# The first products, the step sizes, the memory tokens and the attention pieces of a hybrid decoder step, put in another order

## The chip, the cores and the metric

The kernel runs on one core of one Trainium2 chip. The metric is the device time of one execution in microseconds (us). The core has TensorE (PE, the matrix engine, with its weight loads PEld), VectorE (DVE), ScalarE (ACT), GpSimd (POOL) and SyncE (SP), which here only issues DMA transfers. ACT issues some transfers too. Each engine works through its own instructions in order, and waits at an instruction until what it reads or overwrites is free.

## The reference

One layer of a decoder is computed for 1024 prompt tokens and 8 sample tokens, all in fp32. One normalised input goes through one wide projection; its columns feed three mixers whose results are gated and summed.

```python
def mixer_block(xn, mem_k, mem_v, ...):
    sc_b, sc_c, sc_x, z, xbc, dt_raw, q, gates = jnp.split(xn @ w_in, splits, axis=-1)
    conv_u, sc_new = causal_depthwise_conv(sc_c * sc_x, sc_hist, sc_conv_w)
    y_a = (sc_b * conv_u) @ w_sc_out
    xbc_c, ssm_conv_new = causal_depthwise_conv(xbc, ssm_hist, ssm_conv_w)
    xbc_c = jax.nn.silu(xbc_c + ssm_conv_b)
    xs, bm, cm = jnp.split(xbc_c, ...)
    dt = jax.nn.softplus(dt_raw + ssm_dt_bias)
    a = -jnp.exp(ssm_a_log)
    y_ssd, ssm_new = ssd_fn(xs, dt, a, bm, cm, ssm_s0)
    y_ssd = (y_ssd + ssm_d[:, None] * xs) * jax.nn.silu(z)
    y_b = group_rmsnorm(y_ssd, ssm_norm_w, SSM_GROUPS) @ w_ssm_out
...
```

The third mixer is cross-attention of 4 heads of 256 into 256 memory tokens; for the prompt, keys and values are projected from the normalised `mem_prompt`, for the samples they come from a cache. `xbc` has 24 blocks of 128 columns: 16 of x, four B (block 16 is "B0") and four C (block 20 is "C0"). `dt_raw` has 32 columns, one step size for each head.

## The kernel before

Tokens lie along the free dimension, TT = 1032 = 1024 + 8, features along the 128 partitions. A factor is kept as a high part in the matmul's format and a low part (`weights`, `split_act`), and a product is the sum hi·hi, hi·lo, lo·hi. `gemm` makes one block of 128 output columns from 8 blocks of input as 72 matmuls of 344 columns (rows with L203 in the profile). A pair of blocks can instead be made by Strassen's scheme (`strassen`, matmuls of 258 columns at L248, results named Z2m, X17m, G16m and so on); it needs sums of blocks of the activations (`make_forms`) and of the weights, and splits each into high and low parts: a weight sum such as X17sa is made on DVE in two steps (L315, L316) and cast on ACT (X17Sh, L235).

The instructions are written by functions in program order and then ordered by a scheduler with its own estimates of their durations. Within a `gemm` or a Strassen pair small pieces of other work are issued: the queue `pend` holds them, and `tick` takes one out; `pace` says how many are taken in one gemm. `flush` issues what is left. Tiles come from pools with a fixed number of buffers: three raw weights, five wide tiles in the pool "ev" (`ev_tile`), two PSUM banks for small results (`sm_ps`). A load into a buffer waits until the last reader of the old contents is done, and on SP's queue everything behind it waits too.

The stages that the change touches, in order of time:

- **First phase** (loop at L507). Blocks of x are squared, transposed (ps_xt), scaled into `xw` and split into `xn`. `first_products(g3, k)` (L489) adds block k of the column group g3 to two results at once: ps_dt, the step sizes before the bias (128 weight columns, of which 32 are wanted), and ps_B0. Three products each make 24 matmuls per block row and 72 for each result. Weight blocks are loaded ahead of x3 to x7.
- **Histories** (L522 to L533). The convolution states are loaded and turned by 32 small transposes (ps_h) into `h_xc` and `h_sc`.
- **C0, B0, z0.** dtr takes ps_dt plus the bias on DVE (L553). `xbc_tile(16, "B0")` evicts ps_B0 and starts its convolution; C0 is a gemm of its own inside `xbc_tile(20)`; then `z_step(0)`. Into these gemms five pieces of `pend` are put: a gap, `dt_softplus` (nine transposes ps_dtT, then some twenty DVE steps of 288 columns), `dt_sums` (ps_ac), `dt_rows` (ps_acT, stores to DRAM) and `dt_sample` (ps_ex).
- **Memory tokens.** They are loaded into "ev" tiles, squared on ACT, scaled on DVE (L1172), transposed (ps_mt, L1179) and split in `mem_t`. `kv_block` makes keys and values in 16 pieces inside z1 and the pairs Z2 to Z12; they are stored to k_d and v_d in DRAM.
- **Later pairs**: X17, X18, X19 with B and C blocks, then X and gate pairs, into which `with_steps` puts slots of the sample's recurrence; at the end z_pair(14) and gate_pair(16) with slots, then gate_pair(18), (20), (22).
- **The SSD stage** (groups 0 to 3), with the query products and the first output products as `fillers` and `outs`. `group_norm` ends each group (psny at L1049, psnr, yb_d stores at L1076).
- **Attention**, as pieces within the output products po13 to po27 (`out_part`, one gemm each). `kv_in(m)` loads vv and kk from v_d and k_d and turns kk (pskT). `a_load`, `a_scores` (psa), `a_probs` (psp), `a_out` (psv) work on the prompt's heads. For the samples `s_query`, `s_keys`, `s_scores` take eight samples through DVE, five slots of pieces for each; after the last head come `s_softmax` (pss_sc), `s_probs` (pss_pT), for each sample `s_values` (two loads vc of 512 KB) and `s_out` (pso, 32-column stationary tiles on four column groups, L1484; then a copy so and four stores to os_d), four `conv_state` pieces, and `s_back` (osr, psob, a store into at_d). Then po30 starts, which reads all of at_d back (`in`, cast to b00h at L162).

## Time and profile before

| what | us |
|---|---|
| times of three runs | 2502.51, 2506.6, 2508.41 (median 2506.6) |
| profiled execution, its own time | 2510.98 |
| its span | 2509.3 |
| TensorE busy | 2463.0 |
| VectorE busy | 1518.3 |
| ScalarE busy | 1047.5 |
| mean granted TensorE clock, first phase (0 to 62.44) | 0.99 of full |
| the same, 62.44 to 77.18 | 0.83 of full |

In rows of the timeline the columns are start, duration, engine, line, operation, output <- inputs, shapes and how many were put together (x8); in square brackets stands how long the engine sat idle before it and what ended that. fp32 matmuls other than the split products leave two records each. Matmuls overlap, so the pitch from one start to the next tells more than the duration of one.

### The profile page before, as it was taken

Reading aid. Unit: us, or ns where it says so; the run is one execution under the profiler, and the core shown is the slowest. Engines: PE = TensorE matmul, PEld = TensorE weight load, DVE = VectorE, ACT = ScalarE, POOL = GpSimd, SP = SyncE. Lnnn points to the kernel's source line nnn. Section 1 sums busy time; section 2 is a strip of 40 time slices with the busy share of each in tenths; the row PEclk is TensorE's granted clock in tenths of the full one; section 3 lists DMA queues with packets and bytes.
Section 4 is the critical chain, followed back from the end, with each engine's and each line's share of the span. In section 5 each row is a group of like instructions: output and inputs, shape, how many; then the busy total and the mean of one; then the engine's idle time right before and its main releaser. Section 6 shows DMA issues by size and latency. Waiting matters only on the chain.

```text
span 2509.3 us, 44975 instructions
## 1 busy us (share of the span) xinstructions
PE 2463.0 (98%) x18762; PEld 2398.2 (96%) x18762; DVE 1518.3 (61%) x2484; ACT 1047.5 (42%) x1694; POOL 128.2 (5%) x163
## 2 busy tenths in 40 slices
PE   7999999999999999999999999999999999999998
PEld 5999999999999999999898998899999999999998
DVE  6754586777677764567786672555775445453325
ACT  6554455454545534655554541223443333341212
POOL 0300000000000000211211000000000000000000
PEclk9999999999999999999999999999999999999999
DMA  6344434344344445677886787945443222282211
GB/s 199 112 144 156 131 102 145 110 141 125 98 135 135 130 132 165 194 231 264 264 282 208 242 291 239 305 151 173 136 152 98 89 68 85 81 278 88 68 34 68
DMA packets 348331, 392.08 MB, mean 156 GB/s; under 512 B 15335, under 2 KB 285783, under 8 KB 348120
## 3 DMA queue, kind: packets, MB, share of 16 engines
q1 hardware_dynamic: 327678, 331.50, 42.3%
q10 hardware_dynamic: 20449, 57.71, 6.0%
q8 instruction: 147, 2.41, 0.4%
q14 instruction: 57, 0.46, 0.1%
HBM read 280.40 MB, written 108.98 MB: 155 GB/s over the span
## 4 chain that ended last, share of the span: by engine, by line
PE 89%; DMA 4%; DVE 2%; ACT 2%; issue 1%; SPq 0%; ACTq 0%; POOL 0%; DVEq 0%
PE po L203 13%; PE pd L203 9%; PE pm L1693 4%; PE ps_q L203 2%; PE pss L949 1%; PE py L936 1%; PE po L928 1%; PE ps_z L203 1%; PE u20m L248 1%; PE C3m L248 1%; PE Z6m L248 1%; PE g20m L248 1%; PE u18m L248 1%; PE g18m L248 1%; PE u16m L248 1%
## 5 line engine op out<-in xcount | busy, mean ns | idle before, releaser
L1835 DVE TENSOR_TENSOR x<-pd,x 128x1032 f32<-128x1032 f32 x24 | 29.6, 1232 | 134.4 <-PE pd L203 134.3
L881 ACT ACTIVATE r<-r,acum 128x128 f32<-128x128 f32 x256 | 78.9, 392 | 5.7 <-DMA r<-ac_d 5.2
L661 DVE SCALAR_TENSOR_TENSOR ax<-u,prm,ax 128x1024 f32<-128x1024 f32 x44 | 56.3, 1280 | 0.1
L913 POOL TENSOR_TENSOR xdd<-xdt,decst 128x512 f32<-128x512 f32 x32 | 36.2, 1130 | 320.7 <-DVE xdt L909 320.7
L822 ACT ACTIVATE st<-st,es 128x128 f32<-128x128 f32 x128 | 42.0, 394 | 23.5 <-DMA st<-in_state_ssm_dram 21.7
L1340 DVE TENSOR_TENSOR yr<-po,yr 128x1032 f32<-128x1032 f32 x8 | 9.8, 1230 | 58.7 <-PE po L203 54.6
L907 DVE TENSOR_TENSOR r<-r,cbm 128x1024 f32<-128x1024 f32 x32 | 39.1, 1223 | 2.3 <-ACT r L882 0.2
L824 DVE SCALAR_TENSOR_TENSOR st<-sr,dts,st 128x128 f32<-128x128 f32 x128 | 40.1, 345 | 0.4
L932 DVE TENSOR_TENSOR y<-po,ea 128x512 f32<-128x512 f32 x28 | 19.3, 688 | 28.0 <-PE po L928 25.1
L828 DVE SCALAR_TENSOR_TENSOR sr<-st,sr 128x128 f32<-128x128 f32 x128 | 35.4, 286 | 1.1
L949 PE MATMUL pss<-xdd,bT 128*128 128x512 f32 x64 | 34.2, 616 | 1.0 <-ACT bT L906 0.8
L936 PE MATMUL py<-r,xdt 128*64 128x128 f32 x512 | 35.0, 279 | 0.0
L882 ACT ACTIVATE r<-r 128x1024 f32<-128x1024 f32 x32 | 33.9, 1059 | 0.6
L962 POOL TENSOR_TENSOR s<-s,cdec 128x512 f32<-128x512 f32 x28 | 33.1, 1181 | 2.5 <-DVE s L955 2.2
L1700 DVE TENSOR_TENSOR x<-pm,xT 128x516 f32<-128x516 f32 x16 | 11.1, 695 | 36.3 <-PE pm L1693 36.3
L906 ACT COPY bT<-bp 128x128 f32<-128x128 f32 x32 | 8.5, 265 | 54.8 <-DVE cbm L904 54.7
L936 PEld LDWEIGHTS py<-r,xdt 128*64 128x64 f32 x512 | 27.3, 136 | 4.2 <-issue 0.9
L928 PE MATMUL po<-bc,s 128*128 128x128 f32 x224 | 29.9, 276 | 0.0
L1622 DVE TENSOR_TENSOR gt<-po,gt 128x1032 f32<-128x1032 f32 x8 | 9.9, 1233 | 32.8 <-PE po L203 31.8
L928 PEld LDWEIGHTS po<-bc,s 128*128 128x128 f32 x224 | 28.2, 191 | 0.7 <-DVE s L955 0.5
L1073 DVE SCALAR_TENSOR_TENSOR x<-x,prm,sqa 128x1032 f32<-128x1032 f32 x16 | 19.6, 1290 | 15.0 <-ACT sqa L1069 15.0
L664 DVE SCALAR_TENSOR_TENSOR ax<-u,prm,ax 128x1032 f32<-128x1032 f32 x22 | 28.3, 1287 | 0.0
(9205 smaller groups left out, 8974.3 us busy)
## 6 DMA issues: line engine op xcount, KB each, us to landing
r<-ac_d SPq DMA_DIRECT2D x32, 512.0 KB
gt_d<-G ACTq DMA_DIRECT2D x24, 516.0 KB
gt<-gt_d SPq DMA_DIRECT2D x24, 516.0 KB
xs_d<-ax ACTq DMA_DIRECT2D x22, 516.0 KB
hr<-h_d SPq DMA_DIRECT2D x22, 516.0 KB
x<-xs_d SPq DMA_DIRECT2D x16, 516.0 KB
zs<-zs_d SPq DMA_DIRECT2D x16, 516.0 KB
yb_d<-x SPq DMA_DIRECT2D x16, 516.0 KB
```

The costliest lines, as they stand in the source:

```text
L203: PE.matmul(ps[:, n, :CW], wt[:, ks], x[:, n * CW : (n + 1) * CW], start=(k == 0 and i == 0), stop=(k == nk - 1 and i == 2),)
L248: PE.matmul(ps[:, n, :HC], wt[:, ks], x[:, n * HC : (n + 1) * HC], start=(start and kt == 0 and i == 0), stop=(kt == 3 and i == 2), skip_g ...
L661: V.scalar_tensor_tensor(acc[:, :T], u[:, j : j + T], w[j], acc[:, :T], op0=ALU.mult, op1=ALU.add)
L822: S.activation(st[:, i], st[:, i], AF.Copy, scale=es[:, g * 4 + i, b : b + 1])
L824: V.scalar_tensor_tensor(st[:, i], rb, dts[:, g * 4 + i, b : b + 1], st[:, i], op0=ALU.mult, op1=ALU.add)
L881: S.activation(r[:, j, :], r[:, j, :], AF.Relu, scale=-1.0, bias=acum[:, c, h : h + 1])
L907: V.tensor_tensor(r, r, bc(cbm.unsqueeze(1), [P, HPG, P]), op=ALU.mult)
L913: G.tensor_tensor(b3(xdd, HPG), b3(xdt, HPG), bc(decst[:, c, hs].unsqueeze(2), [P, HPG, 64]), op=ALU.mult)
L928: PE.matmul(po[:, t * P : (t + 1) * P], state["s"][:, t * P : (t + 1) * P], bcg[1][:, cs], start=True, stop=True,)
L936: PE.matmul(py[hp : hp + 64, (h // 2) * P : (h // 2 + 1) * P], xdt[:, h * 64 : (h + 1) * 64], r[:, (h % 2) * 4 + h // 2, :], start=True, s ...
L949: PE.matmul(pss, bT, xdd, start=True, stop=True)
L1693: PE.matmul(ps[:, n, :HC], wt[:, ks], x[:, half * HT + n * HC : half * HT + (n + 1) * HC], start=(k == 0 and i == 0), stop=(k == KD - 1 an ...
```

## The change

Eight edits, in the order of the kernel:

1. The first phase makes B0 and C0; the step sizes are made apart by `step_sizes`, from the raw fp32 weight and the unsplit `xw`: for each column group eight matmuls with 32 stationary columns, block k on the column group k mod 4 of the array, so that the 128 result rows hold four partial sums. ACT adds the bias (on the first 32 rows) and evicts.
2. `dt_turn` turns them with nine fp32 matmuls against `fold`, four identities of 32 below each other, which also adds the four partial sums.
3. Only the last eight blocks of the SSM convolution state are turned at first; the other 24 small transposes, softplus, sums, rows and sample pieces follow after keys and values, in z_pair(14) and gate_pair(16). Those two stand ahead of X17 now, and gate_pair(18) and (20) take their slots of the sample's recurrence.
4. B0 and C0 are convolved one after the other, and z0 and z1 follow without the C0 gemm between.
5. The memory tokens get their own tiles; squares come early, the scaling is on ACT, `mem_block(0)` follows z1 and `mem_block(1)` is a piece in Z2.
6. `kv_ahead` asks for vv0 and kk0 in a slot of the last group norm, and for vv1 and kk1 behind `kv_in(0)`.
7. A sample's query, keys and scores take four slots of pieces instead of five. Softmax, values and results of the samples and the convolution states are put among the remaining pieces of the heads rather than behind them.
8. The probabilities and results of the samples use "ev" tiles, and the pace is computed with one and a little less output product than there are.

```diff
-    ps_dt, ps_b0 = mm_ps("ps_dt"), mm_ps("ps_B0")
+    ps_b0, ps_c0 = mm_ps("ps_B0"), mm_ps("ps_C0")
...
-        w_dt = weights(wblock(w_in, C_DT), "wdt")
         w_b0 = weights(wblock(w_in, C_XBC + 16 * P), "wB0")
+        w_c0 = weights(wblock(w_in, C_XBC + 20 * P), "wC0")
+        w_dt = load_raw(wblock(w_in, C_DT), "wdt")
+        bias = cn.tile([P, 1], F32, tag="bias", name="bias")
+        V.memset(bias, 0.0)
+        SY.dma_start(bias[:HEADS], a["ssm_dt_bias"].rearrange("l h -> h l"))
...
-            for ps, (wh, wl) in ((ps_dt, w_dt), (ps_b0, w_b0)):
+            for ps, (wh, wl) in ((ps_b0, w_b0), (ps_c0, w_c0)):
...
+
+        def step_sizes(g3):
+
+            cw = slice(g3 * CW, (g3 + 1) * CW)
+            ps = sm_ps(f"ps_dt{g3}")
+            for k in range(KD):
+                q = k % 4
+                PE.matmul(
+                    ps[q * HEADS : (q + 1) * HEADS, :CW], w_dt[:, k * P : k * P + HEADS], xw[k][:, cw],
+                    start=(k < 4), stop=(k >= 4),
+                )
+            if g3 == 0:
+                dtr.append(ev_tile("dtr"))
+            S.activation(dtr[0][:, cw], ps[:, :CW], AF.Identity, bias=bias)
...
+            if g3:
+                step_sizes(g3 - 1)
         for k in range(KD):
             first_products(2, k)
+        step_sizes(2)
...
+    def history(key, dst, q0, t):
+        nr = dst.shape[2]
+        SY.dma_start(t, a[key][0].rearrange("b j c -> (b j) c")[:, q0 * P : (q0 + 8) * P])
+        ps = sm_ps(f"ps_h{nr}_{q0}")
+        for i in range(8):
+            PE.transpose(ps[:, i * nr : (i + 1) * nr], t[:, i * P : (i + 1) * P], ident[:nr, :nr])
+        V.tensor_copy(dst[:, q0 : q0 + 8, :].rearrange("p a b -> p (a b)"), ps[:, : 8 * nr])
+
+    history("state_ssm_conv", h_xc, 16, ev_tile("hist", (24, D)))
...
     W = 9 * HEADS
...
+    x0 = ch.tile([P, W], F32, tag="x0", name="x0")
+    fold = ch.tile([P, HEADS], F32, tag="fold", name="fold")
+    V.tensor_reduce(fold, ident.rearrange("p (q h) -> p h q", q=4), axis=AX.X, op=ALU.add)
     dt_flat = dtT.rearrange("p c h -> p (c h)")
 
-    def dt_softplus():
+    def dt_turn():
         ps = sm_ps("ps_dtT")
         for c in range(NCK):
-            PE.transpose(ps[:, c * HEADS : (c + 1) * HEADS], dtr[:, c * P : (c + 1) * P], ident[:HEADS, :HEADS])
-        PE.transpose(ps[:NS, 256:288], dtr[:, T:TT], ident[:HEADS, :HEADS])
+            PE.matmul(
+                ps[:, c * HEADS : (c + 1) * HEADS], dtr[0][:, c * P : (c + 1) * P], fold, start=True, stop=True
+            )
+        PE.matmul(ps[:NS, 256:288], dtr[0][:, T:TT], fold, start=True, stop=True)
...
     pa_ = {"u": ev_tile, "s": lambda nm: ev_tile(nm, (P, 1024))}
-    pend.extend([None, dt_softplus, dt_sums, dt_rows, dt_sample])
+    pend.append(dt_turn)
...
-    w_c0 = weights(wblock(w_in, C_XBC + 20 * P), "wC0")
-    xbc_tile(16, "B0", ps_b0)
-    make_forms(0)
-    xbc_tile(20, "C0", w=w_c0)
-    make_forms(2)
-    z_step(0)
-    flush()
-    dt_stack.close()
...
+    mem_sb = [pm.tile([P, D], F32, tag=f"m{i}1", name=f"mem{m}") for m, i in enumerate("hl")]
+    for m in range(2):
+        SY.dma_start(mem_sb[m], a["mem_prompt"][0, m * P : (m + 1) * P, :])
...
-    def mem_rms():
-        for m in range(2):
-            junk = memT[m][0].rearrange("p k c -> p (k c)")
             S.activation(junk, mem_sb[m], AF.Square, accum_out=mst[:, m : m + 1])
         rsqrt(pm, mrs, mst, D, [P, 2], "m")
         for m in range(2):
-            V.tensor_scalar(mem_sb[m], mem_sb[m], mrs[:, m : m + 1], None, op0=ALU.mult)
-
-    def mem_t(m, half):
-        hi, lo = memT[m]
+            S.activation(mem_sb[m], mem_sb[m], AF.Copy, scale=mrs[:, m : m + 1])
+
+    def mem_turn(m, half):
         ps = sm_ps(f"ps_mt{m}{half}")
         for k4 in range(4):
             k = half * 4 + k4
             PE.transpose(ps[:, k4 * P : (k4 + 1) * P], mem_sb[m][:, k * P : (k + 1) * P], ident)
+        return ps
+
+    def mem_split(m, half, ps):
...
+
+    def mem_block(m):
+
+        pss = [mem_turn(m, half) for half in range(2)]
+        if m == 1:
+            memT.append(mem_tiles(1))
+        for half in range(2):
+            mem_split(m, half, pss[half])
...
-    mem_load()
-    pend.extend([None, mem_rms, None])
-    pend.extend(lambda m=m: [mem_t(m, half) for half in range(2)] for m in range(2))
+    xbc_tile(16, "B0", ps_b0)
+    xbc_tile(20, "C0", ps_c0)
+    make_forms(0)
+    make_forms(2)
+    pend.extend([None, mem_rms])
+    z_step(0)
+    z_step(1)
+    mem_block(0)
+    pend.extend([None, lambda: mem_block(1)])
     pend.extend(lambda j=j, q=q: kv_block(j, q) for j in range(8) for q in range(2))
-    z_step(1)
...
     mem_stack.close()
+    dt_stack = ExitStack()
+    pd_ = dt_stack.enter_context(tc.tile_pool(name="pdt", bufs=1))
+    mx, u, z, z2, q, da, ach = dt_tiles()
+
+    def wide(n):
+        return pd_.tile([24, D], F32, tag="wide", bufs=2, name=n)
+
+    pend.extend([dt_softplus, lambda: history("state_ssm_conv", h_xc, 0, wide("h0")), dt_sums])
+    z_pair(14)
+    pend.extend([
+        dt_rows, dt_sample,
+        lambda: [history("state_ssm_conv", h_xc, 8, wide("h1")), history("state_conv", h_sc, 0, wide("h2")[:16])],
+    ])
+    gate_pair(16)
+    assert not pend
+    dt_stack.close()
...
-    with_steps(3, lambda: z_pair(14))
-    with_steps(2, lambda: gate_pair(16))
+    with_steps(3, lambda: gate_pair(18))
+    with_steps(2, lambda: gate_pair(20))
     assert not steps
-    gate_pair(18)
-    gate_pair(20)
...
+
+    def kv_ahead(m):
+        vv, kk = kv_load[m] = [ev_tile(f"{n}{m}", (P, D)) for n in ("vv", "kk")]
+        SY.dma_start(vv, v_d[m])
+        SY.dma_start(kk, k_d[m])
+
...
+        norm = group_norm(g, xg, hold)
+        if g == GROUPS - 1:
+            norm[1] = lambda: kv_ahead(0)
+        pend.extend(z_pieces(g, xg, hold) + [None] + norm)
     pace[:] = len(pend) / (len(fillers) + KD + 2) + 1e-6, 0.0
...
-            vv = ev_tile(f"vv{m}", (P, D))
-            SY.dma_start(vv, v_d[m])
+            vv, kk = kv_load.pop(m)
             S.copy(vh[:, m, :], vv)
             V.tensor_sub(vl[:, m, :], vv, f32(vh)[:, m, :])
-            kk = ev_tile(f"kk{m}", (P, D))
-            SY.dma_start(kk, k_d[m])
             for half in range(2):
...
+            pr = ev_tile("prs", (P, MEM)).unsqueeze(1)[:32]
             softmax(pr, ps[:32, :MEM], 1, 32, "s")
...
-            t = at.tile([P, 2, MEM], F32, tag="pr", bufs=3, name=f"so{b}")[:, 0]
+            t = ev_tile(f"so{b}", (P, MEM))
...
-        pieces = [[(kv_in, 0)], [(kv_in, 1), (a_load, 0)], [], []]
+        pieces = [[(kv_in, 0), (kv_ahead, 1), (a_load, 0)], [(kv_in, 1)], [], []]
...
+
+        at_ = 2
         for b in range(NS):
-            at_ = 3 + 5 * b
-            for i, fs in enumerate(
-                ([(s_query, b), (s_keys, b, 0)], [(s_keys, b, 1)], [], [(s_scores, b, 0)], [(s_scores, b, 1)])
+            for fs in (
+                [(s_query, b), (s_keys, b, 0)], [(s_keys, b, 1)], [(s_scores, b, 0)], [(s_scores, b, 1)]
             ):
-                pieces[at_ + i].extend(fs)
+                pieces[at_].extend(fs)
+                at_ += 1
+        at_ += 1
+        late = [[(s_softmax,), (s_values, 0)], [], [(s_probs,)], []]
+        for b in range(NS):
+            late += [[(s_out, b)], [(states[b],)] if b < 4 else []]
+        late += [[], [(s_back,)]]
+        pieces.extend([] for _ in range(at_ + len(late) - len(pieces)))
+        for i, fs in enumerate(late):
+            pieces[at_ + i].extend(fs)
 
...
-        pieces = [lambda fs=fs: run(fs) for fs in pieces]
-        pieces += [s_softmax, lambda: s_values(0), s_probs, None]
-        for b in range(NS):
-            pieces += [lambda b=b: s_out(b), None]
-        pend.extend(pieces)
-        pend.extend(states)
-        pend.extend([None, s_back])
-        pace[:] = len(pend) / (len(outs) - 1) + 1e-6, 0.0
+        pend.extend(lambda fs=fs: run(fs) for fs in pieces)
+        pace[:] = len(pend) / (len(outs) - 1.4) + 1e-6, 0.0
```

52 lines of the change are left out of this document (15 added, 37 removed).

## The prediction

> **What bounds the kernel now.** First the page: its share of busy time and its chain of work.
>
> ```profile
> span 2509.3 us, 44975 instructions
> ...
> PE 2463.0 (98%) x18762; PEld 2398.2 (96%) x18762; DVE 1518.3 (61%) x2484; ACT 1047.5 (42%) x1694; POOL 128.2 (5%) x163
> ...
> PE 89%; DMA 4%; DVE 2%; ACT 2%; issue 1%; SPq 0%; ACTq 0%; POOL 0%; DVEq 0%
> ```
>
> TensorE is busy 98% of the span and carries 89% of the chain. A change can therefore win in three ways only: fewer matmuls, a shorter wait of TensorE, or fewer microseconds at a low clock. The second view lists TensorE's waits by what ended them (us in total, times, longest).
>
> ```profile
> PE ps_mt L1179 <- DVE mem L1172: 1.8, 1, 1.8
> ...
> PE pss_sc L1460 <- ACT ot L1561: 1.5, 1, 1.5
> ...
> PE ps_kv L1203 <- DVE meml L1184: 0.8, 1, 0.8
> ...
> PE pso L1484 <- DMA vc<-in_cache_mem_v_dram: 0.3, 1, 0.3
> ```
>
> These four lie where the diff works, and so do the list's waits of 2.12 us before C0, 3.35 before pskT and 4.38 before po30, whose own rows follow below. No row of this view names X17, so its start has no wait now. The third view gives stretches: length, busy time of each engine, granted clock (0.50 is half).
>
> ```profile
> 60.71:67.54 6.83, 5.10 (x18) 5.09 (x18) 6.83 (x13) 4.57 (x6) 4.46 (x1) 0.50 0.28 77
> ...
> 1378.26:1385.08 6.82, 5.88 (x24) 5.91 (x25) 4.94 (x5) 5.51 (x7) 0.00 (x0) 0.50 1.05 343
> 1593.30:1600.12 6.82, 5.64 (x19) 5.45 (x20) 6.07 (x5) 5.00 (x5) 0.00 (x0) 0.50 0.90 324
> 1357.78:1361.19 3.41, 3.41 (x14) 3.41 (x13) 0.17 (x1) 0.00 (x0) 0.00 (x0) 0.50 0.38 156
> ...
> 130.00:133.41 3.41, 2.58 (x22) 2.58 (x23) 2.73 (x6) 2.79 (x7) 0.00 (x0) 1.00 0.19 79
> ...
> 62.44:77.18 14.74, 14.74 (x83) 14.44 (x84) 14.74 (x29) 7.71 (x10) 13.13 (x3) 0.83 0.19 66
> 77.18:101.84 24.66, 24.15 (x152) 23.46 (x151) 21.59 (x38) 16.23 (x21) 10.80 (x2) 1.00 0.32 108
> ```
>
> Half clock comes in pieces of 3.41 us, each costing about 1.7 us of a busy TensorE. It stands around the waits of 2.1, 3.3 and 4.4 us, once with no wait at all, and not at the wait of 1.75 us near 130. So a wait of some 2 us or more is to be charged twice.
>
> **The first phase and C0.** TensorE's timeline around the separate C0 product:
>
> ```profile
> 57.79 0.32 PE L497 MATMUL ps_B<-xnh,wB0l 128*128 128x344 f32 x1
> 58.04 2.28 PE L532 MATMUL ps_h<-ident,hist 24*128 24x24 f32 x32
> 62.44 0.94 PE L203 MATMUL ps_C<-xnh,wC0h 128*128 128x344 f32 x2 [2.12 <-DVE dtr L553]
> ...
> 67.77 0.68 PE L567 MATMUL ps_dtT<-ident,dtr 32*128 32x32 f32 x8
> ...
> 69.46 0.63 PE L203 MATMUL ps_C<-xnh,wC0l 128*128 128x344 f32 x3
> 69.93 0.64 PE L203 MATMUL ps_C<-xnh,wC0h 128*128 128x344 f32 x3
> ...
> 77.02 0.64 PE L203 MATMUL ps_z<-xnh,wz0h 128*128 128x344 f32 x3
> ```
>
> Three matmuls of 344 columns start 0.47 us apart, 0.158 each; 72 of them are 11.4 us. In the changed kernel C0's 72 take the place of dt's 72 in the first phase, and z0 follows. The new step sizes are 24 fp32 matmuls on four column groups. The trace has this form in pso, 64 matmuls recorded as 128:
>
> ```profile
> 1519.16 0.63 PE L203 MATMUL po<-b07h,wo22l 128*128 128x344 f32 x3
> 1519.73 1.07 PE L1484 MATMUL pso<-vc,pTs 128*32 128x256 f32 x16
> 1520.73 0.74 PE L203 MATMUL po<-b00h,wo23h 128*128 128x344 f32 x3
> ```
>
> Eight of 256 columns take from 1519.63, where the next product was due, to 1520.73: 1.10 us. Scaled to 344 columns that is 1.48, and 4.4 us for three blocks. Of 32 small transposes only 8 stay here (2.28 x 8/32 = 0.6). The other 24 move behind the keys and values, where their 1.7 us come back: +1.7. One raw weight more is loaded ahead of x3 (512 KB); I charge 0.4, with 0 to 2.6 as bounds (2.6 is 512 KB at 199 GB/s, the page's first slice). The last product ended about 57.79 + 0.16 = 57.95, so z0 starts at 57.95 + 4.4 + 0.6 + 0.4 = 63.35 instead of 77.02: -13.7, and with the 1.7 **-12.0**, between -16.4 (step sizes wholly in waits that the phase has anyway) and -9.8.
>
> **The turn of the step sizes.** Nine transposes become nine fp32 matmuls against the folded identity. The nearest fp32 matmuls with few columns are those of L1049, nine recorded as 18:
>
> ```profile
> 1354.60 2.06 PE L1049 MATMUL psny<-ones,sqa 128*128 128x1 f32 x18
> 1356.52 0.72 PE L203 MATMUL po<-b05h,wo12l 128*128 128x344 f32 x3
> ```
>
> 1.92 us for nine; the transposes (0.68, row above) are the lower bound. The old ones lay inside the interval that has gone, so the whole 1.9 is added. The last four wait for ACT's eviction of the third block, which stands on ACT's queue behind the Square of the first memory tile, and so behind that tile's DMA: 0.5 us, bounds 0 and the 2.1 for which TensorE waits for dtr now. Right after the psny row the clock fell to half without a wait (1357.78), so I add 0.8 of a possible 1.7. **+3.2**, between +0.7 and +5.7.
>
> **Start of Z2 and the memory tokens.** Now: 1.75 (ps_mt) and 0.77 (ps_kv), and the 0.51 by which TensorE's 24.15 falls short of 24.66 in the last stretch: 3.0 us of waits. z0 and z1 stand back to back before Z2, 2 x 11.4 + 1.9 = 24.7 us of TensorE, and hide VectorE's convolutions of B0 and C0 and the Strassen sums. VectorE is busy 36.3 us in the two stretches above.
>
> ```profile
> 80.86 1.95 DVE L576 RECIPROCAL z<-z 128x288 f32<-128x288 f32 x1
> ...
> 88.76 0.45 DVE L581 SCALAR_TENSOR_TENSOR q<-q,z 128x288 f32<-128x288 f32 x1
> 89.14 0.69 DVE L1117 TENSOR_TENSOR raw<-xw,xw 128x516 f32<-128x516 f32 x1
> ```
>
> Softplus leaves it: the reciprocal (1.9) and sixteen steps like L581 (0.38 each), 8.0. Of the rest four T3 splits, 2.4 at the 0.6 of a 516-column step, are not needed when Z2 starts. 25.9 against 24.7: TensorE waits 1.2 at Z2. For the memory tiles, whose scaling now stands on ACT, it waits up to as long as now. I take 2.0 left (0 to 5): **-1.0**, between -3 and +2.
>
> **The moved step-size work and X17.** Softplus, sums and sample rows ride in Z14 and G16 at unchanged cost, under TensorE. The end of the chain is not covered. In the order of the changed kernel VectorE has, ahead of X17's first sum, the copies of both late histories; the last waits for the eight transposes ps_h16. After these, four products later, TensorE needs the cast of X17's finished sum. The steps from rows of before:
>
> ```profile
> 60.92 0.28 DVE L533 COPY h_sc<-ps_h 128x128 f32<-128x128 f32 x1
> ...
> 308.38 0.69 DVE L316 TENSOR_TENSOR X19sa<-X19sa,X19r 128x512 f32<-128x512 f32 x1
> 308.99 0.69 DVE L331 TENSOR_TENSOR u<-X18m,u 128x516 f32<-128x516 f32 x1
> ```
>
> Copy 0.28, half sum 0.61, a sum of G16's kind (L331) 0.61, half sum 0.61, and ACT's cast of 1024 columns 1.05 (the cast b00h, also 1.05, ends the wait for po30 below): 3.16. Four products of 258 columns cover 0.47 of it. A wait of 2.7 us, charged with one half-clock piece: **+4.4**, from 0 (if the transposes come early) to +6.1 (two pieces). On the same queue the sums of X17's second form and the low parts stand behind it, but these have products between.
>
> [...]
>
> **Attention.** Keys and values are asked for in advance. SP's queue, then TensorE at the first wait and at the end:
>
> ```profile
> 1364.78 3.93 SPq L1076 DMA_DIRECT2D yb_d<-x  x4
> ...
> 1369.60 0.55 SPq L1408 DMA_DIRECT2D kk<-k_d  x1
> 1370.20 1.32 SPq L1404 DMA_DIRECT2D vv<-v_d  x1
> 1371.57 0.42 SPq L1408 DMA_DIRECT2D kk<-k_d  x1
> ```
> ```profile
> 1374.82 1.04 PE L1413 MATMUL pskT<-ident,kk 128*128 128x128 f32 x8
> 1379.20 1.94 PE L1413 MATMUL pskT<-ident,kk 128*128 128x128 f32 x8 [3.35 <-DMA kk<-k_d]
> ...
> 1584.49 0.66 PE L1501 MATMUL psob<-ident,osr 8*128 8x8 f32 x8
> ...
> 1594.48 1.23 PE L203 MATMUL po<-b00h,wo30h 128*128 128x344 f32 x3 [4.38 <-ACT b00h L162]
> ```
>
> The second kk landed at 1379.2, 7.6 us after its issue, behind the four yb_d stores, kk0 and vv1. Afterwards kk0 and vv1 are issued ahead of the stores, and kk0 is turned within po13; kk1 waits for these transposes to free its slot and still goes out behind the stores, at about 1369.6. With less ahead of it, 7.6 us give 1377.2 at the worst; TensorE asks at 1375.9, when the eight transposes of kk0 and po13 are done, as now. I leave 1.0 us of wait, too little for half clock: -(3.35 - 1.0) and -2.9, which is half of the busy 5.88 us of that half-clock stretch. **-5.2**, between 0 (kk1 as late as now) and -6.2.
>
> The wait of 1.5 before pss_sc goes when the sample's scores are taken among the pieces of the last head, as the softmax does not wait for the last eviction any more: **-1.2** (0 to -1.5). At the end, from psob's start it takes 9.99 us until po30 may begin (copy, store and reload of at_d, cast). psob stood 30 products before the end of po27, now 55: 55 x 0.158 + 0.6 = 9.3 us of cover against 30 x 0.158 + 0.6 = 5.3 now (nearly the row's 4.38 is left of it). 0.7 stays, and half clock goes, 2.8: **-6.5**, between -3.7 (half clock stays) and -7.2. For new waits, the sample's values and states being squeezed in between: **+1.0** (0 to 3).
>
> **Sum.** -12.0 + 3.2 - 1.0 + 4.4 - 5.2 - 1.2 - 6.5 + 1.0 = -17.3 us. The profiled execution took 2510.98 us, its span plus 1.7, and is 4.4 above the median of 2506.6; a profile of after would take 2493.7, the median 2489.3.
>
> **Rivals.**
> - The X17 wait does not appear (the histories land and are turned early enough): for it, VectorE's copies are short; against it, the order on its queue is fixed. 2489.3 - 4.4 = 2484.9. Chance 0.13.
> - The new attention slots only move the waits. For it: kk1 still goes out behind the four stores, and the at_d chain has to fit into 9.3 us while 324 to 343 GB/s of loads are moved at both places (third view). Terms 5.2, 1.2 and 6.5 go, and the 1.0 too: 2501.2. Chance 0.19.
> - The four column groups don't overlap in a product of 128 rows: 4.4 becomes 17.7, -4.0 in all, 2502.6. The pso row speaks against it. Chance 0.03.
> - Slower: the sample's values come late. Eight pairs of 512 KB loads of vc must land before their pso; the pairs now come each 45 products (7.1 us), with state rows and four small stores of os_d between them on SP. Were seven of them late by 2.1 us, each with one half-clock piece (1.7), that is 26.6 us, and 2515.9. It decides the sign from (17.3 + 5.0) / 7 = 3.2 us for each, its clock included. Against it: today's eight, nearly as close, wait 0.3 us in all (list of waits). Chance 0.09.
>
> **Numbers.** My forecast has 0.56. Its own range is 2483 to 2496. A measurement can't tell less than about 0.2% from no change, here 2501.6 to 2511.6. Faster is the forecast (0.56), the X17 rival (0.13) and two thirds of the second, which lies at the bound (0.13): 0.82; within 0.2%: the rest of the second and the third, 0.09; slower 0.09. For 8 in 10, the range reaches over both neighbours and no further: 2480 to 2502.
>
> **What would show it.** In the profile after: no separate ps_C group of L203 and z0's first row near 63; step-size rows of about 1.5 us each, three times; ps_dtT near 1.9 us; a wait of X17m on an ACT cast X17Sh between 2 and 3.5 us, with half clock beside it; pskT's wait at or below 1.5 us; at po30 below 1. The forecast is wrong if z0 starts after 66, if the step sizes cost over 3 us a block, or if any pso waits for vc for more than 2 us more than once.

## The result and the profile after

| | before | after |
|---|---|---|
| median of 20 runs each, us | 2507.35 (2502.51 to 2512.18) | 2497.86 (2495.19 to 2504.62) |
| ratio, 95% interval | | 0.9967 (0.9960 to 0.9973) |
| profiled execution, us | 2510.98 | 2497.5 |
| granted clock in it | 0.994 | 0.998 |

The change gains 0.33%, which is 8.3 us of 2507.35 (6.8 to 10.0), where 17.3 were forecast: the sign and the wider range (2480 to 2502) held, the size and the forecast's own range (2483 to 2496) did not. The two profiled executions differ by 13.5 us, more than the runs do, and that is part of the story. The page of the changed kernel, span, busy time and shares of the chain of work:

```profile
span 2495.8 us, 44935 instructions
...
PE 2450.1 (98%) x18747; PEld 2384.2 (96%) x18747; DVE 1515.0 (61%) x2482; ACT 1051.8 (42%) x1698; POOL 118.7 (5%) x163
...
PE 88%; DMA 5%; DVE 4%; ACT 2%; issue 1%; POOL 0%; SPq 0%; ACTq 0%; DVEq 0%
```

TensorE still sets the time. Its waits in the changed kernel, by what ended them (us in total, times, longest):

```profile
PE psa L1568 <- ACT pr L1488: 4.3, 2, 2.7
PE X17m L248 <- ACT X17Sh L235: 2.6, 1, 2.6
...
PE Z2m L248 <- ACT z L770: 1.2, 1, 1.2
...
PE po L203 <- ACT b00h L162: 0.8, 1, 0.8
PE po L203 <- ACT yr L1372: 0.7, 1, 0.7
...
PE pso L1526 <- DMA vc<-in_cache_mem_v_dram: 0.4, 2, 0.2
```

The waits for C0, the memory tokens and pss_sc are gone, and po30's fell from 4.4 to 0.8, with 0.4 and 0.3 behind it. X17 waits, as forecast. The first line was not forecast: the scores of the third head (head 2) wait 4.3 us for exponentials on ACT. The first phase of the changed kernel on TensorE's timeline:

```profile
24.01 0.55 PE L481 MATMUL ps_xt<-ident,x 128*128 128x128 f32 x3 [2.23 <-DVE xw L465]
...
63.85 1.36 PE L510 MATMUL ps_dt<-xw,wdtr 128*32 128x344 f32 x16
65.15 0.67 PE L549 MATMUL ps_h<-ident,hist 24*128 24x24 f32 x8
65.75 0.73 PE L203 MATMUL ps_z<-xnh,wz0h 128*128 128x344 f32 x3
...
66.48 1.20 PE L576 MATMUL ps_dtT<-fold,dtr 128*128 128x32 f32 x10
...
68.07 0.75 PE L576 MATMUL ps_dtT<-fold,dtr 128*128 128x32 f32 x6
68.75 0.23 PE L579 MATMUL ps_dtT<-fold,dtr 128*8 128x32 f32 x2
```

z0 starts at 65.75 instead of 77.02. A block of step sizes takes 1.30 us (63.85 to 65.15). One after the other, four times the prediction's 1.48, it would be 5.9, so the four column groups do run at the same time. The turn takes 1.9 us in its two stretches between products of z0, without a wait for dtr. The wait at 24.01 (0.90 at 22.47 before) is 1.3 us longer.

How X17's wait comes about, from the timeline of all engines:

```profile
313.55 0.66 PE L549 MATMUL ps_h<-ident,h 16*128 16x16 f32 x8
...
314.25 0.29 DVE L550 COPY h_sc<-ps_h 128x128 f32<-128x128 f32 x1 [1.76 <-PE ps_h L549]
314.46 0.68 DVE L315 TENSOR_TENSOR X17sa<-X17r 128x512 f32<-128x512 f32 x1
...
315.67 0.68 DVE L316 TENSOR_TENSOR X17sa<-X17sa,X17r 128x512 f32<-128x512 f32 x1
316.38 1.05 ACT L235 CAST X17Sh<-X17sa 128x1024 fp32r<-128x1024 f32 x1 [0.66 <-DVE X17sa L316]
...
317.48 0.80 PE L248 MATMUL X17m<-T10ah,X17Sh 128*128 128x258 f32 x2 [2.58 <-ACT X17Sh L235]
```

It is the chain of the prediction, row by row: transposes, copy, two half sums with u's sum between them, cast, and then the product.

How the scores of head 2 come to wait:

```profile
1438.65 1.07 ACT L162 CAST b01h<-in 128x1032 fp32r<-128x1032 f32 x1
1442.85 1.06 ACT L162 CAST b02h<-in 128x1032 fp32r<-128x1032 f32 x1 [3.14 <-DMA in<-yb_d]
1446.40 1.05 ACT L162 CAST b03h<-in 128x1032 fp32r<-128x1032 f32 x1 [2.49 <-DMA in<-yb_d]
1447.36 0.47 ACT L1488 ACTIVATE pr<-psa,mx 128x256 f32<-128x256 f32 x1
...
1448.43 0.39 PE L1568 MATMUL psa<-kTh,q20h 128*128 128x256 f32 x1 [2.73 <-ACT pr L1488]
```

Between po17 and po20 ACT casts the next part of the input (b00h to b07h) while that is still being transferred, and the exponentials of head 2 stand behind these casts: their last input, mx, was done at 1445.25, but ACT stood idle until b03h's part had landed, made that cast at 1446.40 and took the exponentials at 1447.36. ACT idles 5.6 us here for yb_d, and TensorE waits for ACT. Edits 6 to 8 have brought head 2 to this place: before, no score waited more than 0.4 us, e1_front, which lacks these edits, has no such wait, and e2_att, which has them alone, shows it:

```profile
PE psa L1533 <- ACT pr L1453: 3.8, 2, 2.8
```

### The profile page after: what moved, and what is told of

Read it like the earlier page. It is cut to its first block, busy times and chain, and to the rows that moved or that the text cites. A ratio compares the mean times of both kernels' runs of the same rounds, so it can differ in the third digit from the quotient of the medians.

```text
span 2495.8 us, 44935 instructions
## 1 busy us (share of the span) xinstructions
PE 2450.1 (98%) x18747; PEld 2384.2 (96%) x18747; DVE 1515.0 (61%) x2482; ACT 1051.8 (42%) x1698; POOL 118.7 (5%) x163
## 4 chain that ended last, share of the span: by engine, by line
PE 88%; DMA 5%; DVE 4%; ACT 2%; issue 1%; POOL 0%; SPq 0%; ACTq 0%; DVEq 0%
PE po L203 12%; PE pd L203 9%; PE pm L1739 4%; PE ps_q L203 3%; PE py L953 1%; PE pss L966 1%; PE po L945 1%; PE X17m L248 1%; PE Z2m L248 1%; PE G16m L248 1%; PE B6m L248 1%; PE C1m L248 1%; PE Z6m L248 1%; PE Z4m L248 1%; PE Z12m L248 1%
## 5 line engine op out<-in xcount | busy, mean ns | idle before, releaser
L1918 ACT ACTIVATE fj<-psy 128x512 f32<-128x512 f32 (+1 forms) x18 | 10.7, 596 | 41.9 <-PE psy L1916 41.8
L677 ACT ACTIVATE ax<-u,prm 128x1024 f32<-128x1024 f32 x22 | 27.4, 1247 | 1.9 <-DVE u L344 0.9
```

## The experiments

Ratios are to the kernel before, run on the same chip; 0.1% is 2.5 us.

### The two halves: e1_front and e2_att

e1_front has the part of the diff ahead of the attention, e2_att the rest. The lines that separate them:

```diff
 e1_front, against the kernel before
-    ps_dt, ps_b0 = mm_ps("ps_dt"), mm_ps("ps_B0")
+    ps_b0, ps_c0 = mm_ps("ps_B0"), mm_ps("ps_C0")
...
+    pend.extend([dt_softplus, lambda: history("state_ssm_conv", h_xc, 0, wide("h0")), dt_sums])
+    z_pair(14)
```
```diff
 e2_att, against the kernel before
+            norm[1] = lambda: kv_ahead(0)
...
-        pieces = [[(kv_in, 0)], [(kv_in, 1), (a_load, 0)], [], []]
+        pieces = [[(kv_in, 0), (kv_ahead, 1), (a_load, 0)], [(kv_in, 1)], [], []]
...
-        pace[:] = len(pend) / (len(outs) - 1) + 1e-6, 0.0
+        pace[:] = len(pend) / (len(outs) - 1.4) + 1e-6, 0.0
```

> The kernel before with the first five edits alone: raw step-size weight in four column groups, C0 with B0, the turn of the step sizes and the memory tokens in their new places, histories, softplus and sums in the new stretch; the attention as before. The prediction's terms for this half were -12.0 + 3.2 - 1.0 + 4.4 = -5.4 us. The profile of the changed kernel has the state-space stage begin at 1005.2 us instead of 1008.4, so theory 1 (each term holds wherever it is run, and the half-clock pieces inside them too) gives -3.2 us. Theory 2 (the profiled execution of the kernel before was a slow one, 3.6 us above its median, and the loss of clock in it, two of its eight half-clock pieces lying in this half at 60.71 to 67.54, is not in the typical run) gives -3.2 + 3.4 = about 0 us. Shown by the time: under -2 us speaks for theory 1, over -1 us for theory 2.

> The kernel before with the last three edits alone: values and keys loaded ahead, four slots in the attention, softmax, values and outputs in the same pieces, the pace; the first phase and the start as before. The prediction's terms for this half were -5.2 - 1.2 - 6.5 + 1.0 = -11.9 us; the two profiles have it at -9.2 from the start of the state-space stage to the output products of tile 30, and -10.3 to the end. Theory 1 (the terms hold) -10 us. Theory 2 (six of the eight half-clock pieces of before's profiled execution lie in this half, 10.2 us by the clock, and only some of them are in a typical run): -5 us. If the two halves hang on each other in the queues, their sum differs from the whole, -8.3 us by the ratio, by more than 2 us.

Measured: e1_front 0.9995 (0.9986 to 1.0004), -1.3 us, with -3.5 as the most that the interval allows; e2_att 0.9981 (0.9972 to 0.9990), -4.8 us. The sum is -6.1 against -8.3 for the whole. The 2.2 between them are just over the 2 us that were to show that the halves hang on each other, but well inside the intervals, so that stays open. Both gained less than the prediction's -5.4 and -11.9. e1_front lies between its two theories, and e2_att is where theory 2 put it. Its mean clock is 0.9972 over 11 runs; that of e1_front is 0.9954, the same as that of the 25 runs of before in this comparison.

### X17: e3_x17 and e12_x17

```diff
-    pend.extend([dt_softplus, lambda: history("state_ssm_conv", h_xc, 0, wide("h0")), dt_sums])
+    pend.extend([
+        dt_softplus,
+        lambda: [history("state_ssm_conv", h_xc, q0, wide(f"h{q0 // 8}")) for q0 in (0, 8)],
+        lambda: [history("state_conv", h_sc, 0, wide("h2")[:16]), dt_sums()],
+        dt_rows,
+    ])
     z_pair(14)
-    pend.extend([
-        dt_rows, dt_sample,
-        lambda: [history("state_ssm_conv", h_xc, 8, wide("h1")), history("state_conv", h_sc, 0, wide("h2")[:16])],
-    ])
+    pend.append(dt_sample)
     gate_pair(16)
```

> The changed kernel with all histories, the sums and the rows in the pieces behind the z products of tiles 14 and 15, and only the sample rows behind the gate products of tiles 16 and 17. Theory: the wait of 2.58 us ahead of the X17 products at 317.48, and the half clock behind it (317.03 to 320.44, 1.7 us), come from the last histories, whose copies on VectorE stand ahead of the sum X17sa; without them the time falls by 4.3 us, to -12.6 us against the kernel before. Rival: the sample rows (the last copies of which run on VectorE at 308.86) or the weight's transfer are late next, a wait of some 2 us moves to another product and the gain is under 1 us. Second rival: the histories come no earlier than X16's conversions and make the z stretch wait, and the time is higher than the changed kernel's.

> The kernel of e3 again, beside e11. Theory: -0.55 to -0.6 % against the kernel before, as in e3 (0.9943), so that the histories moved out of the last stretch are worth 5 to 6 us against the changed kernel, more than the 2.6 us of the wait and the 1.7 us of the half clock. Rival: e3 was a favourable sample and it is 4 us (0.9950 to 0.9955).

Measured: e3_x17 0.9943 (0.9930 to 0.9955), e12_x17 0.9952 (0.9939 to 0.9964): on average -13.2 us, 4.9 below the changed kernel. The same chain in e12_x17:

```profile
308.10 0.17 DVE L662 COPY dpar<-ps_ex 128x16 f32<-128x16 f32 x1
308.19 0.68 DVE L315 TENSOR_TENSOR X17sa<-X17r 128x512 f32<-128x512 f32 x1
308.90 0.69 DVE L316 TENSOR_TENSOR X17sa<-X17sa,X17r 128x512 f32<-128x512 f32 x1
...
309.67 1.05 ACT L235 CAST X17Sh<-X17sa 128x1024 fp32r<-128x1024 f32 x1 [0.75 <-issue]
...
311.07 0.40 PE L248 MATMUL X17m<-T10ah,X17Sh 128*128 128x258 f32 x2
```

The sum starts 6.3 us earlier, behind the sample rows, and no wait stands before the product. The edit moves the sums and `dt_rows` as well, but the rows of the changed kernel show that it is the copy of the last history that the sum stands behind. The term (4.4 us, clock included) was sized about right: against the changed kernel, which was measured in another comparison, it is 6.0 us in e3_x17 and 3.7 in e12_x17. e12_x17 came out where its rival put it (0.9950 to 0.9955, e3 a favourable sample), so "more than the two together" is not established.

### The third weight load: e4_wdt

```diff
-        w_dt = load_raw(wblock(w_in, C_DT), "wdt")
...
             load_x(i)
         SY.dma_start(xs_sb, a["x_sample"][:, 0, :])
+        w_dt = load_raw(wblock(w_in, C_DT), "wdt")
```

> The changed kernel with the load of the step-size weight issued behind the loads of the remaining rows of x. Theory: this third weight load of 512 KB in front of x3 is what makes the first products wait 2.23 us at 24.01 instead of 0.90 at 22.47, and behind it the half-clock piece at 40.55 to 43.97; without it -1.3 us if the wait alone goes and -3.0 us if the half clock goes too, against the changed kernel (-9.6 to -11.3 against the kernel before). Rival: the rows of x are bound by the DMA engines' total and arrive when they did; no change (-8.3 us against before), or the step sizes at 46.90 wait for their weight and the time rises by up to 2 us.

Measured: 0.9970 (0.9960 to 0.9981), -7.5 us: no gain. The wait is where it was:

```profile
23.88 0.55 PE L481 MATMUL ps_xt<-ident,x 128*128 128x128 f32 x3 [2.18 <-DVE xw L465]
```

So moving this load behind the rows of x does not shorten the wait. What the wait stands behind is in the rows of ACT, of before and of the changed kernel: ACT copies the transposed x into a buffer `xt` whose old contents are still being stored (`xT_d`), and VectorE's xw follows that copy.

```profile
21.29 1.01 ACT L457 COPY xt<-ps_xt 128x384 f32<-128x384 f32 x2 [1.00 <-DMA xT_d<-xt]
```
```profile
22.83 1.02 ACT L462 COPY xt<-ps_xt 128x384 f32<-128x384 f32 x2 [2.45 <-DMA xT_d<-xt]
```

In e4_wdt the weight is asked for later, but still ahead of these stores on SP's queue, and ACT waits 2.49 us for them:

```profile
13.85 0.38 SPq L124 DMA_DIRECT2D wdtr<-in_w_in_dram  x1
14.33 3.36 SPq L463 DMA_DIRECT2D xT_d<-xt  x3
```

So the stores land later than before. Whether the third load is what delays them was not tested.

### The same kernels profiled again: e5_before and e6_after

> The kernel before, once more. The times of the 25 runs of it in the first experiments fall with the granted clock: 2509.9 us at 0.994 (2 runs), 2507.8 at 0.995 (12), 2505.6 at 0.996 (9), 2504.6 at 0.997 (2), mean clock 0.9954. The prediction was read from an execution at 0.994, in which 27.3 us before the last stage ran at half clock in five pieces of 3.4 or 6.8 us. Theory (which wait is followed by a half-clock piece, and how long, changes from one execution to the next): the waits stand where they stood (2.1 at C0, 3.4 at pskT, 1.5 at pss_sc, 4.4 at tile 30, within 0.4 us), but the half-clock pieces are others, at most three of the five at the same waits, and their sum is under 27 us. Rival (the pieces belong to the waits): the same five pieces within 2 us of their places and a time of 2509 to 2511 us.

> The changed kernel, once more. Its first profiled execution had a clock of 0.998, the highest of its 20 runs (mean 0.9964), and two half-clock pieces, 6.8 us in all. Theory (the pieces change from one execution to the next): the waits stand as they stood (2.6 at X17, 2.7 and 1.6 at the scores of head 2, 0.8 at tile 30, within 0.5 us each, in sum within 1 us), and more half-clock time than 6.8 us appears, some of it at waits that had none, or at the small transposes of the sample rows at 304 to 308. Rival: the same two pieces and 2495 to 2498 us.

Measured: e5_before 2510.94 us at 0.994, e6_after 2498.41 at 0.997. In e5_before the waits stood as they stood, except that pskT's fell from 3.35 to 2.45 and pss_sc's rose from 1.47 to 2.08. In e6_after X17's, po30's and the first at the scores did; the second at the scores fell from 1.59 to 0.28, and waits of 1.1 us came ahead of psp and at pso. The theory on the pieces failed for e5_before: four of the five came back within 0.1 us of their places (60.65, 1183.64, 1378.20, 1593.24), one of them shorter, and only that at 1357.78 was replaced, by one at 1507.90; the time is the rival's, too. For e6_after it held: pieces at 23.79, 317.34 and 1447.15, the first and the last new. What stands ahead of some of the pieces, and of some places without one, is in the next rows. In each row: stretch, length, busy time of TensorE, of its weight loads, VectorE, ScalarE and GpSimd, then the granted clock. The four fences are e5_before, the changed kernel (first profile), e11_pace26 and e12_x17; the last two kernels are described in their own places:

```profile
1374.79:1378.20 3.41, 1.29 (x11) 1.02 (x9) 2.35 (x4) 3.41 (x5) 0.00 (x0) 1.00 0.80 292
1378.20:1381.61 3.41, 3.08 (x13) 3.11 (x14) 2.38 (x4) 2.14 (x4) 0.00 (x0) 0.50 1.02 377
1381.61:1385.03 3.42, 3.42 (x25) 3.42 (x24) 2.58 (x3) 2.31 (x3) 0.00 (x0) 1.00 1.08 317
```
```profile
313.62:317.03 3.41, 1.27 (x13) 1.04 (x12) 2.74 (x5) 2.12 (x5) 0.17 (x3) 1.00 0.00 0
317.03:320.44 3.41, 2.96 (x14) 2.96 (x14) 3.01 (x4) 1.87 (x3) 0.00 (x0) 0.50 0.55 145
1446.84:1450.25 3.41, 1.82 (x14) 1.82 (x15) 1.84 (x8) 3.41 (x8) 0.00 (x0) 1.00 0.88 337
1450.25:1453.67 3.42, 3.42 (x25) 3.40 (x24) 3.33 (x11) 2.86 (x8) 0.00 (x0) 1.00 0.75 220
```
```profile
1445.48:1448.89 3.41, 1.51 (x11) 1.25 (x11) 2.95 (x8) 1.77 (x5) 0.00 (x0) 1.00 1.02 419
1448.89:1452.31 3.42, 3.42 (x14) 3.42 (x13) 3.42 (x13) 3.03 (x8) 0.00 (x0) 0.50 1.03 414
```
```profile
1443.84:1447.25 3.41, 1.74 (x14) 1.74 (x15) 2.27 (x12) 3.41 (x7) 0.00 (x0) 1.00 0.93 284
1447.25:1450.66 3.41, 3.41 (x25) 3.39 (x24) 3.31 (x11) 1.98 (x6) 0.00 (x0) 1.00 0.88 273
```

In the first profile of before the five pieces begin at 60.71, 1183.70, 1357.78, 1378.26 and 1593.30, the later four 329, 380, 386 and 449 times 3.4133 us behind the first. In the 3.41 us ahead of a piece TensorE was at work for 1.29 us (e5_before), 1.27 (the changed kernel, 313.62) and 1.51 (e11_pace26); in two stretches without a piece behind them for 1.82 (the changed kernel, 1446.84) and 1.74 (e12_x17). So the same wait stood with half clock in one execution and without it in another: the first wait at the scores of head 2 has it in e6_after (2.5 us), and not in the first profile of the changed kernel (2.7 us) or in e12_x17 (2.3 us), while a wait of 1.9 us ahead of psp had it in e11_pace26. The two profiles of before have their first piece at almost the same time (60.71 and 60.65). e2_att, the same kernel up to the last group norm, shows of the 6.8 us at C0 3.4 (from 61.16), and a piece at 122.60 that neither profile of before has. Why four pieces of the two profiles of before stand at the same times is open.

### The pace of the attention: e7_pace26, e8_pace34, e10_pace, e11_pace26

```diff
-        pace[:] = len(pend) / (len(outs) - 1.4) + 1e-6, 0.0
+        pace[:] = len(pend) / (len(outs) - 2.6) + 1e-6, 0.0
```

e7_pace26 and e11_pace26 have this on top of e3_x17's edit, e8_pace34 the same with 3.4, e10_pace has the line alone.

> The kernel of e3 (histories out of the last stretch) with the attention's pieces taken a little faster: len(outs) - 2.6 instead of - 1.4 in the pace, so that two of the four softmax blocks of head 2 come ahead of the casts of the next half's input, b00h to b07h, on ScalarE. Theory: the waits at the scores of head 2 (3.7 + 0.2 us in e3, 2.7 + 1.6 in the changed kernel) come from exponentials queued on ScalarE behind casts whose input is still in transfer; with two of the four ahead of them about half goes, -2 us against e3 (-16 us against the kernel before). Rival: the output products behind them wait for the same transfers anyway, and the wait only moves to po20: 0 us. Second rival: with the pieces ahead of the cached values' loads pso waits longer, and it loses up to 2 us.

> As e7, with - 3.4 in the pace: three of the four softmax blocks of head 2 come ahead of b00h, the fourth behind b01h. Theory: nearly all of the 3.9 us goes, -3 to -4 us against e3 (-17 to -18 us against the kernel before), and less than 1 us of wait is left at the scores of head 2. Rival: the transfers' own lateness comes out at po20, 0 us. Second rival: waits at the cached values (pso) or at the other heads' scores take its place, 0 to +2 us.

> The changed kernel with the pace over len(outs) - 2.6 alone, the histories where the change has them. Theory: of the 4.3 us of waits at the scores of head 2 (2.73 and 1.59) about 3 us go and 1.5 us come back ahead of psp, and the window that these waits leave idle goes with them: -2 to -3 us against the changed kernel (-10 to -11 us against the kernel before). Rival: as before the waits only move within the attention, 0 (-8.3 us).

> The kernel of e7 again, beside that of e3 in one comparison, because e7 and e3 differed by less than their intervals. Theory 1 (a wait removed at the scores of head 2 is time gained): -2 us or more against e12. Theory 2 (the output products run no earlier, and the wait is given back in shorter ones): under 1 us. [...]

Measured: e7_pace26 0.9937 (0.9922 to 0.9952) and e11_pace26 0.9945 (0.9932 to 0.9957), against 0.9943 and 0.9952 for e3_x17 and e12_x17: -1.5 and -1.8 us. e8_pace34 0.9942 (0.9930 to 0.9955), -0.2 us against e3_x17. e10_pace 0.9963 (0.9951 to 0.9976), -1.0 us against the changed kernel. Each difference is smaller than its interval. The waits at the scores of head 2 do go; what stands there now in e8_pace34 is

```profile
PE psp L1584 <- ACT pr L1490: 1.7, 1, 1.7
```

Some 4 us of waits became 1.7, and 0 to 2 us of time: about half of what was expected, with the same sign in all four comparisons. The -1.8 of e11_pace26 lies between its two theories, nearer to the first. The gain that e8_pace34 should have had beyond e7_pace26 was not seen. As for the clock, e11_pace26 has four pieces of half clock, at 25.54, 308.84, 1087.08 and 1448.89, and e12_x17 has none ahead of its last stage. In the 3.41 us ahead of that at 1448.89 TensorE was at work for 1.51 us. In the 3.41 us ahead of 308.84 (small transposes) and of 1087.08 (ordinary products and nine of one column) it was at work for all 3.41.

### The loads ahead: e9_noahead

```diff
-            norm[1] = lambda: kv_ahead(0)
...
-            vv, kk = kv_load.pop(m)
+            vv, kk = (ev_tile(f"{n}{m}", (P, D)) for n in ("vv", "kk"))
+            SY.dma_start(vv, v_d[m])
+            SY.dma_start(kk, k_d[m])
```

> The changed kernel with the loads of keys and values back at the pieces that use them (no load ahead; slots, pace and all else as changed). [...] Rival: the slot before it and the two pieces between load and use hide the transfer already, and the load ahead is worth under 1 us (-7.5 to -8.5).

Measured: 0.9975 (0.9965 to 0.9984), -6.3 us, so 2.0 us are lost against the changed kernel, more than the rival's 1 us and less than the 2.5 to 4.5 us that the author had forecast; the intervals overlap. That a wait of 2.4 to 3.4 us always brings half clock was the author's estimate, and no run shows it. Its rows, and under them those of the changed kernel:

```profile
1370.27 1.06 PE L1455 MATMUL pskT<-ident,kk 128*128 128x128 f32 x8 [0.81 <-DMA kk<-k_d]
1373.93 1.23 PE L203 MATMUL po<-b00h,wo14h 128*128 128x344 f32 x3 [2.60 <-ACT yr L1372]
```
```profile
1371.10 1.03 PE L1455 MATMUL pskT<-ident,kk 128*128 128x128 f32 x8
1372.84 0.74 PE L203 MATMUL po<-b00h,wo14h 128*128 128x344 f32 x3 [0.70 <-ACT yr L1372]
```

0.81 + 2.60 = 3.4 us of waits against 0.7, and the three products behind them took 1.23 us instead of 0.74, as the three behind the wait for po30 did in the kernel before (1594.48), where the granted clock was 0.50. Of the waits only the 0.81 ends with kk itself; the 2.60 ends with ACT's copy yr, which in that profile follows, on ACT, the casts of the turned keys and of a query. So the load ahead shortens the waits by about what the prediction said (2.5 us, 2.35 forecast), but of the 5.2 us of its term, clock included, the runs show 2.0, with an interval that reaches from nothing to more than 4.

## Why the prediction was too large

The sum of -17.3 holds -5.75 that are half clock: 2.55 inside the -13.7 of the first phase (half of the 5.10 busy us of its stretch), +0.8 at the turn, +1.7 at X17, -2.9 at pskT, -2.8 at po30. The other -11.55 are work and waits.

**The clock terms were mis-sized.** "So a wait of some 2 us or more is to be charged twice" was the rule of the prediction. The runs do not show it: behind the wait of 2.73 us at the scores of head 2 the granted clock of the changed kernel was 1.00 (1446.84 to 1453.67). The pieces of half clock that were to go did go: no profile with the new front half has one at C0, and none with the new attention has one at po30 or, where the loads are ahead, at pskT. But they were priced at the length that one execution showed, 6.8 us each. The other profiles of the old order have 6.8 and 3.4 us at C0, 3.4 and none at pskT, and 6.8 and 3.4 at po30. And of the pieces that the new order brings, only those at X17 and at the turn were in the sum. X17's stands in all six profiles that have its wait; the turn's in none of eleven. Not in the sum were a piece between 23 and 44 us of the first phase (6 of 11 profiles, none of the three of the old order), one at the small transposes of the sample rows between 306 and 314 us (6 of 11; in the old order, at their old place, 1 of 3), and one at the scores of head 2 (4 of the 7 with that pace). Whether a wait was followed by half clock, and for how long, differed between executions of one kernel (6.8 and 3.4 us at pskT in the two profiles of before), so such a term is a chance.

What the clock brings can only be estimated, because the runs of before beside the changed kernel have no clock on record. The profiled execution of before had 0.994; the 58 runs of it in the four later comparisons have a mean of 0.9957 (0.9954 to 0.9962 by comparison), and 2 of them had 0.994. The changed kernel has a mean of 0.9964 over its 20 runs. In the first experiments the time of before falls from 2509.9 us at 0.994 to 2504.6 at 0.997, 1.8 us for a thousandth; in the other three comparisons it is 0.1 to 2.4. So the clock brings some -1 to -2 us and not -5.75, an estimate.

At the same clock these 25 runs of before and the changed kernel, two comparisons, stand at 2507.8 and 2502.8 (0.995), 2505.6 and 2499.1 (0.996), 2504.6 and 2496.5 (0.997), mean -6.5. e4_wdt, whose edit gained nothing, ran beside these 25 runs and stands 6.2, 3.6 and 6.6 us below them, mean -5.5. So work and waits bring about -5.5 to -6.5, where -11.55 was forecast. The halves divide it otherwise: the front half has the clock of before, as forecast (-2.55 + 0.8 + 1.7 is about nothing), and falls short by 4.1 us through work and waits alone; in e2_att, at 1.8 thousandths more, some 3 of its 4.8 us would be clock. The prediction did take its 4.4 us off at the end, but off both kernels alike, where it belongs to before alone.

**One reading behind that rule was wrong.** The piece at C0 begins at 60.71, and the wait runs from 60.32 to 62.44: the clock fell 0.4 us into the wait. The stretch ahead of it, 57.30 to 60.71, held the 32 small transposes, and TensorE was at work for 3.02 of its 3.41 us. So only 0.4 of the 2.1 us of waiting stand ahead of the piece, and of its two halves only the second begins behind the wait; that the 2.1 us brought it is not shown. Ahead of pskT's piece, from 1374.85 to 1378.26, TensorE was at work for 1.00 us. And two of the five pieces stood without a wait, not one: that at 1183.70 follows nine one-column products psny (1180.70), as that at 1357.78 does.

**The new waits of the attention were mis-sized.** The step was +1.0 (0 to 3) for new waits in the attention. In the profile after they are 2.73 + 1.59 + 0.23 before psa, 0.18 before psp and 0.36 before pso, 5.1 in place of 0.9 at psa and pso before: +4.2. Its cause was not seen: the prediction looked at SP's queue and at vc, which arrives in time, and not at what the exponentials stand behind on ACT. e1_front and e2_att show that the edits of the attention make these waits, e7_pace26 and e11_pace26 that the pace moves them, and that not all of their length is lost time.

**The other steps**, without clock:

| step | predicted | measured in the profiles |
|---|---|---|
| up to z0 | -11.2 | -10.4 (77.02 - 2.55 to 65.75 - 1.71); of the 0.8 between them the wait at 24.01 is 1.3 |
| step sizes | 4.4 | 3.9 |
| 24 histories moved | +1.7 | +1.8 (2.39 us for 32, by pitch) |
| turn | +2.4 | +1.9, no wait for dtr |
| Z2 and memory | -1.0 | -1.9: waits 3.0 to 1.2, the memory tiles wait for nothing |
| X17 | +2.7 | +2.6; removing the cause, clock included, gains 6.0 and 3.7 in two comparisons (4.4 said) |
| pskT | -2.35 | -2.5 (3.35 to 0.17 + 0.70) |
| pss_sc | -1.2 | -1.5 |
| po30 | -3.7 | -2.9 (4.38 to 0.82 + 0.40 + 0.30) |

One more loss has no term. The moved step-size work was to ride "at unchanged cost, under TensorE". The stretch of Z14, G16, X17, X18 and X19 before and after:

```profile
276.37:337.07 60.70, 60.70 (x506) 60.70 (x505) 44.04 (x60) 28.12 (x34) 2.94 (x14) 1.00 0.32 97
906.34:946.81 40.47, 40.47 (x338) 40.47 (x337) 21.43 (x37) 16.82 (x21) 0.00 (x0) 1.00 0.45 142
```
```profile
260.54:374.02 113.48, 110.70 (x911) 108.63 (x910) 76.06 (x115) 60.76 (x84) 4.03 (x17) 0.98 0.32 98
```

It grew by 113.48 - 101.17 = 12.3 us. X17's wait and clock are 4.1, the histories 1.8, the sums, rows and sample rows 3.9 (by pitch, and gone from the stretch after z0). That leaves 2.5 us. By the pitch of the rows they lie between the products themselves: a product of 258 columns takes 0.120 us in the stretches of before, but beside small transposes, which are taken a few at a time, the pitch is 0.21 to 0.23 us, at 14 places (303.44 and 304.24 are two). That is about 1.4 us; the rest has no name, and no run tested it.

So of the 9.0 us that are missing, the clock is some 4 to 5, the new waits 3.2 and this stretch some 2.5; the small terms give back a little. These are estimates from profiles and runs of several comparisons, and they add up to 9 only within a microsecond or so. Of the rivals, the one in which the slots only move the waits was half right, but at head 2 and not at the places that it named. The late vc of the slower case did not come: pso waits 0.4 us in all, 1.5 in e6_after. None of the prediction's signs of being wrong appeared (z0 at 65.75, step sizes at 1.30 a block), because none of them watched the clock or ACT.

## What to carry to other kernels

Work out a change first without the clock, and price the loss of clock as a chance over several executions, for the waits that come as for those that go: one profiled execution can stand at the end of its spread, and a term read from it is then counted in full although it is there only sometimes. When pieces of work are moved closer together, list for every engine, ACT too, what its queue holds at the new place, above all conversions that wait for a transfer. When late work is placed at the end of a stage, look at what shares an engine with it next: putting the histories one pair earlier was worth about half of what the whole change brought (e3_x17 and e12_x17). With the faster pace besides, e7_pace26 and e11_pace26 stand 0.55 to 0.63% below the kernel before, which the intervals do not tell apart from e3_x17 alone.

## What the runs showed of the hardware

- Ahead of the last stage half clock stood in pieces of 3.41 or 6.83 us: in the first profile of before at 60.71 (6.83), 1183.70 (3.41), 1357.78 (3.41), 1378.26 (6.83) and 1593.30 (6.83), in that of the changed kernel at 40.55 and 317.03 (3.41 each).
- In the 3.41 us ahead of a piece TensorE was at work for 1.00 us (from 1374.85, before), 1.27 us (313.62, the changed kernel), 1.29 us (1374.79, e5_before), 1.51 us (1445.48, e11_pace26) and 1.87 us (37.14, the changed kernel). With 1.74 us (1443.84 of e12_x17) and 1.82 us (1446.84 of the changed kernel) none followed, so the rows show no bound between the two.
- A piece stood without a wait too. In e11_pace26 TensorE shows no gap in the first of these two stretches, but in it stand nine one-column products (psny, 18 records):

```profile
1083.67:1087.08 3.41, 3.41 (x29) 3.41 (x28) 0.17 (x1) 1.00 (x1) 0.00 (x0) 1.00 0.83 308
1087.08:1090.49 3.41, 3.41 (x15) 3.35 (x14) 0.72 (x4) 0.50 (x2) 0.00 (x0) 0.50 0.00 1
```

The transposes of 8 rows and columns at 303 to 308 were followed by half clock in e1_front, e3_x17 (3.41 of 3.41 us at work, then 0.50 from 306.35) and four others too, and not in the changed kernel (1.00 from 303 to 308), e6_after, e7_pace26, e8_pace34 or e12_x17.
- In the first half of the 6.83 us pieces of before TensorE was at work for 1.68 (60.71), 2.47 (1378.26) and 2.23 us (1593.30) of 3.41. At the small transposes of e3_x17 the granted clock was 0.50 from 306.35 to 313.18, with TensorE at work throughout.
- Eight fp32 products of 344 columns on four column groups of 32 took 1.30 us together (63.85 to 65.15 of the changed kernel).
